# Adaptive max pooling: each load as one contiguous block of the input, outputs in 4 KB rows

## The chip, the core and the metric

The kernel runs on one core of a Trainium2 chip. The core's VectorE (DVE) does all the arithmetic here; SyncE (SP) and ScalarE (ACT) only issue transfers; 16 DMA engines, shared by all queues of the core, move the data between the memory of the chip (DRAM in the profile's names) and SBUF, the on-chip memory of 128 partitions. The metric is the device time of one execution in microseconds (us), as the median of several runs. The profile is of one execution, and its span goes from the first to the last instruction.

## The reference

The input `x` has the shape 32 x 256 x 4096 in float32 (134.22 MB), and the output 32 x 256 x 256 (8.39 MB). Each output is the maximum of a window of 16 neighbouring inputs:

```python
for i in range(output_size):
    start = int(i * length / output_size)
    end = int((i + 1) * length / output_size)
    result[:, :, i] = np.max(x[:, :, start:end], axis=-1)
```

As 4096 is 16 x 256, the windows neither overlap nor cross a row. The whole input can be seen as one flat list of 2,097,152 windows of 64 bytes, in the order of the outputs. Each of the 128 partitions has to handle 16,384 of them, and which ones it handles is free.

## The kernel before

The kernel works on the flat list of windows (`xw`, line 51) and the flat list of outputs (`ow`, line 52). A number of windows `n` in the code always means `n` per partition: 64 n bytes of input and 4 n bytes of output in each partition.

**Two groups.** The function `group` (line 64) takes the next n x 128 windows of the list and cuts them into 128 equal consecutive pieces, one per partition. Group A holds 13,436 windows per partition, group B the other 2,948. So in group A the data of two neighbouring partitions lies 13,436 x 64 = 859,904 bytes apart in DRAM (the "860 KB" row pitch), and in group B 188,672 bytes.

**Loads.** A group is read in several loads, each a column range of that picture: for every partition one run of up to 65,536 bytes, 128 runs in all, a row pitch apart. There are 17 loads: one of 128 windows (`FIRST`, 8,192 bytes per partition), twelve of 1024 (65,536 bytes) and one of 1020 from group A, then two of 1024 and one of 900 (`last`) from group B. Group A is read from the end of its rows to their start, group B from start to end. All loads are issued by SP (lines 87 and 96), in order, on one queue.

**The ring.** The loads land in the tile `ring`, which has room for two loads of 1024 windows and a little more (`GAP`, 152 windows, for each). A load is reduced by two instructions of DVE (line 101, by the helper `pooled`, whose recorded line is 56): one over 872 windows, then one over 152. In every second pass through the ring a load lies 152 windows further along, so it never covers the 152 windows of the old load that the second instruction reads: it has to wait only for the 872-window instruction of the load two before it. In the steady state there is one load moving and the next one queued behind it.

**Outputs.** The maxima go to the tile `kept`, in which each partition has one row of 15,484 outputs. The maxima of the last load (900 per partition) go into `ring` itself, to a place whose data has been read already. At the end come three stores. ACT stores the 900 last outputs per partition (line 114) when the last reduction is through. SP stores the 13,436 outputs per partition of group A, and then the 2,048 others of group B (line 117). In DRAM the outputs of one partition are consecutive within its group, so these three stores have one run per partition each: 53,744, 8,192 and 3,600 bytes. `tc.no_sync_barrier()` stands ahead of SP's stores so that the stores come behind all loads on SP in the program's order. On SP, the store of group A is issued right behind the last load.

**Order.** SP executes its list strictly in order: a load that waits for DVE holds up all that stands behind it. DVE does the reductions in the order of the loads. The framework puts the semaphore waits in; at the very end SP waits for all outstanding transfers (line 148 in the profile).

Of the kernel before, what the change touches and what calls it, by code (L numbers as in the profile page):

```python
# [1 line left out]

# [4 lines left out]


@with_exitstack
def kernel(  # L10
    ctx: ExitStack,
    tc: tile.TileContext,
    x: bass.AP,
    output_size: bass.AP,
    out: bass.AP,
):

    nc = tc.nc
    P = nc.NUM_PARTITIONS
    fp32 = mybir.dt.float32

    B, C, L = x.shape
    O = int(output_size)  # L30
    assert L % O == 0, (L, O)
    W = L // O
    total = B * C * O // P
    assert B * C * O % P == 0

    CHUNK = 1024
    GAP = 152
    FIRST = 128
    LOADS_A, LOADS_B = 13, 2

    LESS = 4
    group_a = [FIRST] + [CHUNK] * (LOADS_A - 1) + [CHUNK - LESS]
    last = total - sum(group_a) - LOADS_B * CHUNK
    group_b = [CHUNK] * LOADS_B + [last]
    assert 0 < last and last * (W + 1) <= CHUNK * W

    pool = ctx.enter_context(tc.tile_pool(name="pool", bufs=1))
    ring = pool.tile([P, 2 * (CHUNK + GAP) * W], fp32, tag="ring", name="ring")
    kept = pool.tile([P, total - last], fp32, tag="kept", name="kept")

    xw = x.flatten_outer_dims().rearrange("r (o w) -> (r o) w", w=W)
    ow = out.flatten_outer_dims().rearrange("r o -> (r o)")

    def pooled(dst, at, n):

        nc.vector.reduce_max(  # L56
            out=dst,
            in_=ring[:, at * W : (at + n) * W].rearrange("p (n w) -> p n w", w=W),
            axis=mybir.AxisListType.X,
        )  # L60

    taken = 0

    def group(n):

        nonlocal taken
        span = slice(taken * P, (taken + n) * P)
        taken += n
        return (
            xw[span].rearrange("(p n) w -> p (n w)", p=P),  # L70
            ow[span].rearrange("(p n) -> p n", p=P),
        )

    stores = []
    n_loads = 0
    base = 0
    for g, loads in enumerate((group_a, group_b)):
        xg, og = group(sum(loads))
        a = sum(loads) if g == 0 else 0
        for n in loads:  # L80
            if g == 0:
                a -= n
            xn = xg[:, a * W : (a + n) * W]
            dst = kept[:, base + a : base + a + n] if n != last else None
            if n == FIRST:

                nc.sync.dma_start(  # L87
                    out=ring[:, CHUNK * W : (CHUNK + n) * W], in_=xn
                )
                pooled(dst, CHUNK, n)  # L90
            else:

                low = n_loads % 2 * (CHUNK + GAP)
                moved = n_loads // 2 % 2
                at = low + moved * GAP
                nc.sync.dma_start(out=ring[:, at * W : (at + n) * W], in_=xn)
                if n != last:
                    cut = CHUNK - GAP if moved else GAP
                    parts = [(0, cut), (cut, n)]
                    for u, v in parts if moved else parts[::-1]:  # L100
                        pooled(dst[:, u:v], at + u, v - u)
                else:
                    end = (at + CHUNK) * W
                    last_kept = ring[:, end - n : end]
                    pooled(last_kept, at, n)
                n_loads += 1
            if g:
                a += n
        full = a - last if g else sum(loads)
        stores.append((og[:, 0:full], kept[:, base : base + full]))  # L110
        base += full
    assert taken == total

    nc.scalar.dma_start(out=og[:, full : full + last], in_=last_kept)
    tc.no_sync_barrier()
    for dst, src in stores:
        nc.sync.dma_start(out=dst, in_=src)


# [1 line left out]
_INS = ['x', 'output_size']  # L121
_OUTS = [((32, 256, 256), 'float32')]

_NUMBERS = {'output_size': 256}


# [26 lines left out]
```

## Time and profile before

| | us |
|---|---|
| time, median of 3 runs (lowest, highest) | 334.98 (334.96, 335.02) |
| span of the profiled execution | 333.06 |
| DVE busy, 32 reductions | 276.5 |
| DVE idle ahead of a reduction, 16 times, all for a load | 51.5 |
| one reduction of 872 windows per partition | 14.69 |
| one reduction of 152 windows per partition | 2.68 |
| the last reduction, of 900 windows per partition | 15.14 |
| a full load, from issue to landing (median) | 24.0 |

The profiled execution has its span of 333.06 us from the first to the last instruction; a timed run is 1.92 us longer at the median, which is what lies around the span. The DMA engines moved 142.61 MB, 428 GB/s over the span. The profile counts as packets the single contiguous runs (one per partition and transfer here) and the 4-byte writes by which each of the 16 engines counts a transfer's semaphore. The records of the single packets have a size, a start and a duration; each engine handles one packet at a time, and 8 of the 128 runs of a transfer. An "issue to landing" time includes the time that a transfer stands behind others in its queue.

### The profile page before, as it was taken

What the parts mean: (1) busy time and instruction counts of PE and PEld (TensorE: products, weight loads), DVE (VectorE), ACT (ScalarE), POOL (GpSimd) and SP (SyncE); (2) the same over time, 40 slices, a digit from 0 to 9 for tenths busy, and PEclk for the clock granted to TensorE, in tenths of its full rate; (3) what the DMA queues carried; (4) which work ended last, traced back from release to release, by engine and by line L of the source; (5) the groups of instructions that cost most, each with busy time, mean ns of one, the idle gap of its engine ahead of it and who ended that gap; (6) DMA issues with size and microseconds to landing.
All of it is one profiled execution on the core that took longest, in us unless ns stands there. A gap on an engine that the chain in (4) does not pass through costs nothing.

```text
span 333.1 us, 113 instructions
## 1 busy us (share of the span) xinstructions
DVE 276.5 (83%) x32; POOL 0.2 (0%) x4
## 2 busy tenths in 40 slices
DVE  2009979797997979799797979979797998979993
POOL 0000000000000000000000000000000000000000
DMA  9898989899898989899898989899898989899996
GB/s 378 378 504 378 504 378 496 386 441 441 378 504 378 504 378 496 386 457 425 378 504 378 504 378 504 378 441 441 385 494 377 504 378 504 378 458 443 421 413 285
DMA packets 2880, 142.61 MB, mean 428 GB/s; under 512 B 320, under 2 KB 320, under 8 KB 448
## 3 DMA queue, kind: packets, MB, share of 16 engines
q1 hardware_dynamic: 2736, 142.15, 98.8%
q10 hardware_dynamic: 144, 0.46, 0.3%
HBM read 134.22 MB, written 8.39 MB: 428 GB/s over the span
## 4 chain that ended last, share of the span: by engine, by line
DMA 57%; DVE 36%; DVEq 5%; issue 0%; SPq 0%
DMA ring<-in_x_dram 57%; DVE kept L56 36%; DVEq L148 5%; SPq L87 0%
## 5 line engine op out<-in xcount | busy, mean ns | idle before, releaser
L56 DVE TENSOR_REDUCE kept<-ring 128x152 f32<-128x2432 f32 (+3 forms) x31 | 261.4, 8472 | 51.5 <-DMA ring<-in_x_dram 51.5
L56 DVE TENSOR_REDUCE ring<-ring 128x900 f32<-128x14400 f32 x1 | 15.1, 15144 | 0.0
L134 POOL MEMSET const-bfloat16-1.0<- 128x1 bf16 x1 | 0.1, 102 | 0.0
L134 POOL MEMSET const-uint8-127<- 128x1 uint8 x1 | 0.1, 102 | 0.0
L134 POOL MEMSET const-float32-0.0<- 128x1 f32 x1 | 0.1, 99 | 0.2 <-issue 0.2
L134 POOL MEMSET const-float32-1.0<- 128x1 f32 x1 | 0.1, 99 | 0.0
## 6 DMA issues: line engine op xcount, KB each, us to landing
ring<-in_x_dram SPq DMA_DIRECT2D x1, 8160.0 KB, 23.9
ring<-in_x_dram SPq DMA_DIRECT2D x1, 7200.0 KB, 21.6
out_dram<-kept SPq DMA_DIRECT2D x1, 6718.0 KB, 37.2
ring<-in_x_dram SPq DMA_DIRECT2D x1, 1024.0 KB, 4.7
out_dram<-kept SPq DMA_DIRECT2D x1, 1024.0 KB, 18.1
out_dram<-ring ACTq DMA_DIRECT2D x1, 450.0 KB, 4.2
ring<-in_x_dram SPq DMA_DIRECT2D x14, 24.0
```

The costliest lines, as they stand in the source:

```text
L56: nc.vector.reduce_max(out=dst, in_=ring[:, at * W : (at + n) * W].rearrange("p (n w) -> p n w", w=W), axis=mybir.AxisListType.X,)
L134: nc = _bacc.Bacc("TRN2", target_bir_lowering=False, num_devices=1)
L148: with _tile.TileContext(nc) as tc:
```

## The change

The groups go. Each load takes the next consecutive block of the flat list of windows and cuts that block into 128 pieces, one per partition. So a load of 1024 windows reads one block of 8 MB without a gap, and neighbouring partitions' runs are 65,536 bytes apart, each beginning where the one before it ends. The sizes become 128, fifteen times 1024, and 896 (`last`) windows per partition. Loads are still 128 runs of up to 65,536 bytes each, issued by SP in order; the places in the ring, the cutting into 872 and 152 windows and the order of the reductions are as before (`place` and the loop over `LOADS`).

In the output, the maxima of one load of 1024 windows now form one block of 512 KB, in which each partition owns 4,096 bytes. The tile `kept` has the loads' outputs side by side in each partition. A store of several loads thus has one run of 4,096 bytes per partition and load. There are four stores: ACT's of the last load (3,584 bytes per partition); on SP those of the first 13 full loads (13 runs of 4,096 bytes per partition), then of `FIRST` (512 bytes per partition), then of the last two full loads (2 runs of 4,096 bytes per partition). The first of SP's stores stands right behind the last load again.

```diff
-    LOADS_A, LOADS_B = 13, 2
-    LESS = 4
-    group_a = [FIRST] + [CHUNK] * (LOADS_A - 1) + [CHUNK - LESS]
-    last = total - sum(group_a) - LOADS_B * CHUNK
-    group_b = [CHUNK] * LOADS_B + [last]
+    LOADS = 15
+    LATE = 2
+    last = total - FIRST - LOADS * CHUNK
...
-    def group(n):
+    def block(n, many=1):
...
-        span = slice(taken * P, (taken + n) * P)
-        taken += n
+        span = slice(taken * P, (taken + n * many) * P)
+        taken += n * many
         return (
-            xw[span].rearrange("(p n) w -> p (n w)", p=P),
-            ow[span].rearrange("(p n) -> p n", p=P),
+            xw[span].rearrange("(l p n) w -> l p (n w)", p=P, n=n),
+            ow[span].rearrange("(l p n) -> p l n", p=P, n=n),
         )
...
+    xf, of = block(FIRST)
+    nc.sync.dma_start(out=ring[:, CHUNK * W : (CHUNK + FIRST) * W], in_=xf[0])
+    pooled(kept[:, 0:FIRST], CHUNK, FIRST)
+
+    xl, ol = block(CHUNK, LOADS)
+    xe, oe = block(last)
...
+    def place(i):
+        moved = i // 2 % 2
+        return i % 2 * (CHUNK + GAP) + moved * GAP, moved
+
+    for i in range(LOADS):
+        at, moved = place(i)
+        nc.sync.dma_start(out=ring[:, at * W : (at + CHUNK) * W], in_=xl[i])
+        dst = kept[:, FIRST + i * CHUNK : FIRST + (i + 1) * CHUNK]
+        cut = CHUNK - GAP if moved else GAP
+        parts = [(0, cut), (cut, CHUNK)]
+        for u, v in parts if moved else parts[::-1]:
+            pooled(dst[:, u:v], at + u, v - u)
+
+    at, _ = place(LOADS)
+    nc.sync.dma_start(out=ring[:, at * W : (at + last) * W], in_=xe[0])
+    end = (at + CHUNK) * W
+    last_kept = ring[:, end - last : end]
+    pooled(last_kept, at, last)
+
+    nc.scalar.dma_start(out=oe[:, 0, :], in_=last_kept)
     tc.no_sync_barrier()
-    for dst, src in stores:
-        nc.sync.dma_start(out=dst, in_=src)
+    for lo, hi in ((0, LOADS - LATE), (LOADS - LATE, LOADS)):
+        nc.sync.dma_start(
+            out=ol[:, lo:hi, :],
+            in_=kept[:, FIRST + lo * CHUNK : FIRST + hi * CHUNK].rearrange(
+                "p (l n) -> p l n", n=CHUNK
+            ),
+        )
+        if lo == 0:
+            nc.sync.dma_start(out=of[:, 0, :], in_=kept[:, 0:FIRST])
```

More of the change, by code (lines that the diff above doesn't have):

```diff
@@ L62 @@
     taken = 0
-    def group(n):
+    def block(n, many=1):
         nonlocal taken
-        span = slice(taken * P, (taken + n) * P)
-        taken += n
+        span = slice(taken * P, (taken + n * many) * P)
+        taken += n * many
         return (
-            xw[span].rearrange("(p n) w -> p (n w)", p=P),
-            ow[span].rearrange("(p n) -> p n", p=P),
-        )
[L74 to L111, printed above, removed]
@@ L112 @@
-    assert taken == total
-    nc.scalar.dma_start(out=og[:, full : full + last], in_=last_kept)
-    tc.no_sync_barrier()
-    for dst, src in stores:
-        nc.sync.dma_start(out=dst, in_=src)
+            xw[span].rearrange("(l p n) w -> l p (n w)", p=P, n=n),
+            ow[span].rearrange("(l p n) -> p l n", p=P, n=n),
+        )
+    xf, of = block(FIRST)
+    nc.sync.dma_start(out=ring[:, CHUNK * W : (CHUNK + FIRST) * W], in_=xf[0])
+    pooled(kept[:, 0:FIRST], CHUNK, FIRST)
+    xl, ol = block(CHUNK, LOADS)
```

## The prediction

> **What bounds the kernel now.** I read the page's head first, then stretches of the span with their DMA share, then the DMA queues and issues, the order of time at the end, and last the single packet records of the trace, grouped by size.
>
> ```profile
> span 333.1 us, 113 instructions
> DVE 276.5 (83%) x32; POOL 0.2 (0%) x4
> q1 hardware_dynamic: 2736, 142.15, 98.8%
> q10 hardware_dynamic: 144, 0.46, 0.3%
> DMA 57%; DVE 36%; DVEq 5%; issue 0%; SPq 0%
> ```
>
> DVE is busy for 83%, the 16 DMA engines for 99.1%. The chain of waits names DVE for 36%, and that misleads: a load's issue waits for DVE to free half of the ring, but the load before it is still moving then. The stretches show it (columns: stretch, busy us of DVE and POOL, clock, DMA share, GB/s):
>
> ```profile
> 0.00:5.00 5.00, 0.00 (x0) 0.20 (x4) 1.00 1.00 393
> 5.00:290.00 285.00, 240.57 (x28) 0.00 (x0) 1.00 1.00 432
> 290.00:312.00 22.00, 19.93 (x4) 0.00 (x0) 1.00 0.99 424
> 312.00:333.00 21.00, 15.97 (x2) 0.00 (x0) 1.00 0.90 384
> ```
>
> In the loads the DMA share is 1.00 and DVE has room: 17.28 us of work in a period of 19.35 us. Only the last stretch is not full, and that is its end: the last packet ends at 331.7. The order of time at the end, and the issues:
>
> ```profile
> 290.99 0.33 SPq L96 DMA_DIRECT2D ring<-in_x_dram  x1
> 291.37 21.91 SPq L117 DMA_DIRECT2D out_dram<-kept  x2
> 295.63 17.28 DVE L56 TENSOR_REDUCE kept<-ring 128x872 f32<-128x13952 f32 x2 [2.07 <-DMA ring<-in_x_dram]
> 312.82 15.14 DVE L56 TENSOR_REDUCE ring<-ring 128x900 f32<-128x14400 f32 x1
> 328.00 0.37 ACTq L114 DMA_DIRECT2D out_dram<-ring  x1
> ...
> out_dram<-kept SPq DMA_DIRECT2D x1, 6718.0 KB, 37.2
> out_dram<-kept SPq DMA_DIRECT2D x1, 1024.0 KB, 18.1
> out_dram<-ring ACTq DMA_DIRECT2D x1, 450.0 KB, 4.2
> ```
>
> The large store is issued at 291.4, lies behind the last load in the same queue, and moves from 311.9 to 328.2. The second store follows to 330.6 and ACT's last one to 331.7 (its data lands at 332.2). Packet records, each engine having 8 of every 128: 65,536 B takes 2419 ns (median; mean 2420.6, fastest 2415, 1792 of them); 57,600 B 2131 (mean 2150); 53,744 B, a store, 1985; 8,192 B 309; 3,600 B, a store, 141. Summed over all data packets and divided by 16 they give 330.0 us, and from the first packet's start (1.7) to the last one's end (331.7) it is 330.0 us. So the engines never stand still: time before is 1.7 us, plus the sum of packet times, plus 1.4 us to the end of the span. What changes no packet's duration and does not starve the queue changes nothing.
>
> The sum is made against this execution's 333.06 us; the median of the three timed runs, 334.98, is 1.92 us more, and that is carried over. A difference under 0.2%, 0.67 us, cannot be told from no change: "same" is 334.31 to 335.65.
>
> **The change part by part.**
>
> Loads, bytes and rows. Before, per partition: 8,192, 14 x 65,536, 65,280 and 57,600 B; after: 8,192, 15 x 65,536 and 57,344 B. The same bytes in the same 17 packets, issued in the same order on SP behind the same waits on DVE: 0 us.
>
> Loads, row pitch. No load of before has a 64 KB pitch. Two pitches are in the trace: 859,904 B (mean of a load's 65,536 B packets 2419.2 to 2423.3 ns) and 188,672 B (2421.5 in both loads). A pitch 4.6 times smaller moved the packet by under 2 ns, inside the spread of the loads at one pitch. Each engine has 120 such packets, plus 8 nearly as long, so 1 ns on all is worth 0.13 us. Lower end: every packet at the fastest seen, 2415, and FIRST's packets all at 309 (its first 16, from a cold start, took 618 on average, in all 0.42 us per engine too much): -0.72 - 0.42 = -1.1 us. Upper end: each of the 17 loads meets that cold price once per engine, 17 x 0.31 = +5.3 us. I take 0, by the row that is nearest in pitch.
>
> Stores. Before, per engine: 8 x 1986 = 15.89 us, 8 x 311.9 = 2.50 us, 8 x 143 = 1.15 us; 19.53 us in 24 packets. After: 15 rows of 4,096 B per partition, one of 512 B, one of 3,584 B, 136 packets. No 4,096 B packet is in the trace; the line through 3,600 B (141) and 8,192 B (309) gives 159 ns: 120 x 159.1 = 19.10 us. The same line gives 28 ns for 512 B, 8 x 28 = 0.22 us; 3,584 B stays at 8 x 143 = 1.14 us. Sum 20.46, that is +0.93 us. Ends: without any price per packet 4,096 B would take 151 ns (the long packets' 0.0368 ns per byte), which takes 1.0 us off; if all took 17 ns more, as the slowest 3,600 B packet did (158 against 141), it adds 2.0 us. I take 159, because 3,600 B is a store to this same output, and only 14% shorter.
>
> Here a rule is weighed. The rows say that a packet costs 7 to 9 ns beside its bytes (6.9 from 53,744 and 65,536 B, 9.3 from 3,600 and 8,192 B); 112 more packets are 0.77 to 1.04 us, which agrees with the 0.93. The Trainium skill, page "DMA: Bandwidth & Descriptors", section "Why small descriptors are slow (HBM only)", puts about 3 cycles of fixed bus cost on each packet; with the 850 MHz that the page gives for the fabric that is an estimate of 3.5 ns, and 112 packets would add only 0.4 us. The rows here do not bear that out, they show twice as much.
>
> Issue of the stores. Store A now has 128 x 13 = 1664 rows instead of 128. SP's issue of a 128-row DMA takes 0.33 to 0.43 us. For 1664 rows it lies between that and 13 times as much, 5.5 us. I take the upper end, and it costs 0: it begins at 291.4, the queue reaches store A only at 311.9, and behind it on SP stand just the 512 B store (0.4 us) and store B, whose wait for DVE ends at 312.9 anyway. Without this cover it would be 5 us.
>
> A fourth store, one more semaphore. Its completions cost 9 ns per engine. In the closing waits on SP, each step that finds its semaphore set takes 0.067 us (331.124 to 331.191). Store B now lands last, not ACT's store, and its semaphore is likely to be first in that row instead of third: +0.13 us; between 0 and that.
>
> DVE and the tail. The last reduction has 896 instead of 900 outputs: 15.14 x 4/900 = 0.07 us less, off the path: ACT's store is then issued at 327.9, its packets begin some 2.2 us later (as 328.0 to 330.24), and 1.15 us of them alternate with store B's until the engines run out of bytes at 331.7 + 0.9 = 332.6. Some 1.3 us of cover; beyond it each us late is a us on the end.
>
> Sum: 0 + 0.93 + 0.01 + 0.13 = +1.07 us; span 334.1, time 334.98 + 1.07 = 336.05 us, +0.3%.
>
> **The rivals.**
>
> B, the 64 KB pitch slows the loads: 16 engines stand in rows that begin at multiples of one power of two, and meet in the same part of the memory. For it: nothing in the trace excludes it, since both pitches of before are odd multiples of 256 B. Against it: packets sit at one flat duration, 2418 to 2427 for nine in ten, for both. Price: from +0.5 us (4 ns a packet) to +5.3 us (the cold price per load), so 336.6 to 341.4, with half of it at about 338.7. The Trainium skill, same page, section "Latency and other measured facts", reports such a loss for copies with row pitches of 512 KiB (slight) to 8 MiB (half the rate), and names contiguous tiles as a cure; no run here shows either, and its smallest pitch is eight times this one.
>
> C, the packet's own price is smaller than the line says, at 4,096 B under 4.8 ns instead of 7 to 9 (then 112 x 4.8 + 0.13 = 0.67 us), or the loads give half a us back. 334.9 to 335.65, no difference. For it: durations are recorded only to some ns. Against it: three pairs of sizes give 7 ns or more. The page's 3 cycles would end here.
>
> D, the row generator becomes the bound: engines take a 4,096 B row every 159/16 = 9.9 ns; if SP's queue hands them out more slowly than that and cannot store them up during the 20 us before, the end is paced by it. At 12 ns per row 1920 rows add 4 us, at 20 ns 19 us: 340 to 355. Against it: 0.43 us for 128 rows is 3.3 ns per row.
>
> E, the other side: contiguous blocks are read faster. Place: the 65,536 B packets. To end below 334.31 it must bring 1.74 us, 13.6 ns of each of 128 packets, so 2407 ns or less; none of the 1792 was under 2415.
>
> **How the numbers follow.** My forecast A, loads unchanged and 0.8 to 1.0 us more in the stores, has 0.54; its own range, with 0.35 us either way for the loads (2.7 ns, the slowest load's mean), is 335.5 to 336.5, and 0.06 of it lies under 335.65. B has 0.22, C 0.12, D 0.07, E 0.05. Slower: 0.48 + 0.22 + 0.07 = 0.77. Same: 0.06 + 0.12 = 0.18. Faster: 0.05. The range 335.1 to 341.0 leaves out E (0.05), C's lower part (0.03), nearly all of D (0.06) and B's top (0.04): 0.18.
>
> **What would show it.** Right: 65,536 B packets still at 2419, 4,096 B ones at 159, DMA share 1.00 up to about 332.6, DVE's idle time before each load's reduction still 2.07 us. B shows in that idle time growing and in packets over 2425; C in 4,096 B packets at 155 or less; D in a DMA share well under 1.00 after 312 or in store A's issue taking over 20 us; E in packets under 2410. A hole between the last load's packets and store A's, or ACT's store beginning after 331.5, would make the sum wrong at the tail.

## The result, and the profile after

The changed kernel takes 335.75 us (median of 9 runs, 335.43 to 336.01) against 334.98 us (334.88 to 335.12): 0.77 us more, a ratio of 1.0022 with a 95% interval of 1.0013 to 1.0030. The profiled execution of it has a span of 333.64 us against 333.06 and belongs to the quickest of the nine; a second one, of the same kernel, had 333.96.

The changed kernel's page: the head, the DMA queues, the chain, and the issues (KB each, us from issue to landing).

```profile
span 333.6 us, 114 instructions
DVE 276.5 (83%) x32; POOL 0.2 (0%) x4
DMA packets 4688, 142.61 MB, mean 427 GB/s; under 512 B 336, under 2 KB 464, under 8 KB 2512
q1 hardware_dynamic: 4544, 142.15, 99.0%
DMA 57%; DVE 36%; DVEq 5%; issue 0%; SPq 0%
ring<-in_x_dram SPq DMA_DIRECT2D x1, 7168.0 KB, 21.6
out_dram<-kept SPq DMA_DIRECT2D x1, 6656.0 KB, 37.4
ring<-in_x_dram SPq DMA_DIRECT2D x1, 1024.0 KB, 4.9
out_dram<-kept SPq DMA_DIRECT2D x1, 1024.0 KB, 15.4
out_dram<-ring ACTq DMA_DIRECT2D x1, 448.0 KB, 4.6
ring<-in_x_dram SPq DMA_DIRECT2D x15, 24.0
out_dram<-kept SPq DMA_DIRECT2D x1, 64.0 KB, 37.1
```

Nothing has changed in kind: the same bytes, DVE busy as long as before, the chain alike, the full loads still 24.0 us from issue to landing. Of the difference the page shows only 1808 more packets. The stretches of the changed kernel (stretch, busy us of DVE and POOL, clock, DMA share, GB/s) and its end in order of time:

```profile
0.00:5.00 5.00, 0.00 (x0) 0.20 (x4) 1.00 0.72 249
5.00:290.00 285.00, 240.39 (x28) 0.00 (x0) 1.00 1.00 433
290.00:312.00 22.00, 19.92 (x4) 0.00 (x0) 1.00 1.00 429
313.00:328.00 15.00, 15.00 (x2) 0.00 (x0) 1.00 1.02 422
```

```profile
291.23 0.33 SPq L95 DMA_DIRECT2D ring<-in_x_dram  x1
291.61 0.43 SPq L103 DMA_DIRECT2D out_dram<-kept  x1
292.09 24.18 SPq L110 DMA_DIRECT2D out_dram<-kept  x1
295.88 17.28 DVE L53 TENSOR_REDUCE kept<-ring 128x872 f32<-128x13952 f32 x2 [2.08 <-DMA ring<-in_x_dram]
313.07 15.07 DVE L53 TENSOR_REDUCE ring<-ring 128x896 f32<-128x14336 f32 x1
316.31 1.25 SPq L103 DMA_DIRECT2D out_dram<-kept  x1
328.18 0.38 ACTq L100 DMA_DIRECT2D out_dram<-ring  x1
```

Two lines are to be read twice. A DMA share of 1.02 cannot be a share of time: the recorded durations of neighbouring packets overlap. So it is not quite true that each engine handles one packet at a time. Inside a transfer a packet's record begins 3 to 4 ns before the one ahead of it ends, in long packets too: those of 65,536 B begin every 2416 to 2417 ns and are recorded with 2420. (In the first stretch the low share is only a matter of where a few long packets are counted, by their start.) And the 512 B store's issue on SP took 24.18 us, where other issues take 0.33 to 0.43: I read this as a full queue.

For the sizes I read the single packets, and the landing of each transfer, for which each of the 16 engines counts once; "mean" is the mean of the 16 counts, in us from the span's start.

| mean landing of | before | after | after, second profile |
|---|---|---|---|
| the first load (1 MB) | 5.16 | 5.44 | 5.36 |
| the last full load | 295.34 | 295.70 | 295.63 |
| the last load | 312.45 | 312.73 | 312.79 |
| ACT's store, the last of all | 332.01 | 332.59 | 332.67 |
| from the last load to that | 19.56 | 19.86 | 19.88 |
| ACT's store on the slowest engine | 332.20 | 332.79 | 333.11 |

So there are two losses, one at either end: 0.2 to 0.3 us by the time the first load has landed, 0.3 us between the last load and the last store. What lies between takes as long as before: 19.346 us per load before, 19.351 after. The span ends with the slowest engine, not with the mean. In the second profile the slowest is 0.44 us behind the mean at the end, in the two others 0.2; this gap differs from profile to profile (0.15 to 0.54 us in those with pitches up to 840 KB), so single spans are a blunt measure of losses this small.

### The profile page after: what moved, and what is told of

Same layout as the page of the kernel before. It is cut to its first block, busy times and chain, and to the rows that moved or that the text cites. A ratio compares the mean times of both kernels' runs of the same rounds, so it can differ in the third digit from the quotient of the medians.

```text
span 333.6 us, 114 instructions
## 1 busy us (share of the span) xinstructions
DVE 276.5 (83%) x32; POOL 0.2 (0%) x4
## 4 chain that ended last, share of the span: by engine, by line
DMA 57%; DVE 36%; DVEq 5%; issue 0%; SPq 0%
DMA ring<-in_x_dram 57%; DVE kept L53 36%; DVEq L141 5%; SPq L74 0%
## 5 line engine op out<-in xcount | busy, mean ns | idle before, releaser
L53 DVE TENSOR_REDUCE kept<-ring 128x872 f32<-128x13952 f32 (+2 forms) x31 | 261.5, 8474 | 51.7 <-DMA ring<-in_x_dram 51.7
L53 DVE TENSOR_REDUCE ring<-ring 128x896 f32<-128x14336 f32 x1 | 15.1, 15075 | 0.0
```

Of the source, the lines that this page charges most:

```text
L53: nc.vector.reduce_max(out=dst, in_=ring[:, at * W : (at + n) * W].rearrange("p (n w) -> p n w", w=W), axis=mybir.AxisListType.X,)
```

## The experiments

Two theories stood against each other after that. **S**: the whole loss is the price of 112 more store packets. **L**: the packets cost only 0.4 us, and the rest sits in the contiguous loads, most likely in the cold start. Crossing loads and stores of the two kernels tells them apart.

### The changed kernel again

> The changed kernel once more, unaltered, for its spread and a second profile. Both theories: 335.75 us give or take 0.15 (334.98 before). Theory S (all of the loss is the 112 extra store packets, loads are free): its 4,096 B packets recorded at 159 ns, store packets summing to 20.4 us per engine against 19.5 before, and whatever varies from one execution to the next varies there. Theory L (part of the loss sits in the contiguous loads): the first packets from a cold start again near 950 ns instead of 618, first load landing near 5.6 us instead of 5.44, and the full-size loads at 2420 ns as before.

Measured: 335.72 us (335.49 to 335.91, before beside it 334.98). The first 16 packets took 906 ns on average (940 in the first profile, 618 before), the first load landed at 5.49 at the latest and 5.36 on average, the 65,536 B packets stand at 2420.8 ns. The cold start (the first packet of each engine) is slower both times. But L had the first load landing near 5.6 at the latest, and on the slowest engine it is only 0.05 us behind the 5.44 of before; the loss shows in the mean.

### Contiguous loads, long rows in the stores

```diff
-    for lo, hi in ((0, LOADS - LATE), (LOADS - LATE, LOADS)):
-        ...
+    cut = (FIRST + (LOADS - LATE) * CHUNK) * P
+    end = cut + LATE * CHUNK * P
+    long_a = ow[0:cut].rearrange("(p n) -> p n", p=P)
+    long_b = ow[cut:end].rearrange("(p n) -> p n", p=P)
+    nc.sync.dma_start(out=long_a, in_=kept[:, 0 : cut // P])
+    nc.sync.dma_start(out=long_b, in_=kept[:, cut // P : end // P])
```

> The loads of the changed kernel, and stores of long rows as before (53,760 and 8,192 B per partition, and ACT's 3,584 B). The maxima of all loads but the last are stored in another order than the reference has. Theory S: the loss is gone, 334.98 us give or take 0.1. Theory L: 0.2 to 0.4 us stay, 335.2 to 335.4, with the wider spread of the changed kernel, and the first load's packets still cold at about 950 ns.

Measured: 335.15 us (334.79 to 335.51), 1.0004 of before with an interval of 0.9995 to 1.0013. The difference of the medians, 0.17 us, lies just under L's forecast, and the interval alone does not exclude S. The trace does show the head's loss: first load at 5.37, last load at 312.71 (before: 5.16 and 312.45). It is made good at the tail: 19.38 us from the last load to the last store, where before needed 19.56.

### Loads of before, 4 KB rows in the stores

```diff
-    nc.scalar.dma_start(out=og[:, full : full + last], in_=last_kept)
+    n_k, n_e = CHUNK, 896
...
+    nc.scalar.dma_start(out=oe, in_=last_kept[:, 0:n_e])
...
-    for dst, src in stores:
-        nc.sync.dma_start(out=dst, in_=src)
+    for lo, hi, at in ((0, 13, FIRST), (13, 15, base - 2 * n_k)):
+        nc.sync.dma_start(
+            out=ol[:, lo:hi, :],
+            in_=kept[:, at : at + (hi - lo) * n_k].rearrange("p (l n) -> p l n", n=n_k),
+        )
+        if lo == 0:
+            nc.sync.dma_start(out=of, in_=kept[:, 0:FIRST])
```

> The loads of before with the four stores of the changed kernel (4,096 B rows, one of 512 B, 3,584 B from ACT). Four outputs per partition of the last load are not stored and the rest stands in another order than the reference has. Theory S: the whole loss, 335.75 to 335.9 us (7 to 9 ns per extra packet, as the durations say). Theory L: only 0.4 us of it, 335.3 to 335.5, since the 4,096 B packets of the changed kernel follow each other every 155 ns although each is recorded with 159, which leaves 3.5 to 4 ns per extra packet.

Measured: 335.39 us (335.19 to 335.76), 1.0015 (1.0006 to 1.0024) of before. That is +0.41 us, in L's range and below S's, though the upper end of the interval, 335.78, just reaches S's 335.75. The first load landed at 5.18 on average, as before; from the last load to the last store it took 19.90 us.

The two halves, 0.17 and 0.41, add up to 0.58 of the 0.74 to 0.77 us. With intervals of some 0.3 us either way the rest of 0.2 us is not resolved.

### The changed kernel with the first load as before

```diff
-    nc.sync.dma_start(out=ring[:, CHUNK * W : (CHUNK + FIRST) * W], in_=xf[0])
+    far = 13436
+    xs = xw[0 : far * P].rearrange("(p n) w -> p (n w)", p=P)
+    nc.sync.dma_start(out=ring[:, CHUNK * W : (CHUNK + FIRST) * W],
+                      in_=xs[:, (far - FIRST) * W : far * W])
```

> The changed kernel with one difference: the first load of 1 MB reads 8,192 B rows 859,904 B apart, as before, instead of one block. Its outputs belong to other windows than the reference's there. Theory S: no difference to the changed kernel, 335.75 us. Theory L with the cold start as the place: its first 16 packets back at about 620 ns and 0.2 us gained, 335.5 us. Theory L with the 64 KB pitch of the later loads as the place: 335.75 us, too, though the first packets are quicker.

Measured: 335.40 us (335.13 to 336.20) beside 335.72 of the changed kernel on the same chip. The first packets are back at 670 ns and the first load at 5.17. S expected no difference. The runs of the two kernels overlap (335.49 to 335.91 for the changed one), so the 0.32 us between the medians is likely rather than certain. The start of DVE's first reduction shows the same in the orders of time, in this sequence: before, changed kernel, this run, contiguous loads with long rows.

```profile
5.46 2.29 DVE L56 TENSOR_REDUCE kept<-ring 128x128 f32<-128x2048 f32 x1 [5.46 <-DMA ring<-in_x_dram]
```

```profile
5.63 2.29 DVE L53 TENSOR_REDUCE kept<-ring 128x128 f32<-128x2048 f32 x1 [5.63 <-DMA ring<-in_x_dram]
```

```profile
5.49 2.29 DVE L53 TENSOR_REDUCE kept<-ring 128x128 f32<-128x2048 f32 x1 [5.49 <-DMA ring<-in_x_dram]
```

```profile
5.56 2.29 DVE L53 TENSOR_REDUCE kept<-ring 128x128 f32<-128x2048 f32 x1 [5.56 <-DMA ring<-in_x_dram]
```

DVE waits for the slowest of the 16 engines, so this column shows a little less than the mean landings do. The trace of this run does not carry the gain to its end: its third load lands at 44.19 on average (changed kernel 44.13 and 44.06), and its last load at 312.80 (312.73 and 312.79). In this one execution something slower in between used up the head start; the gain rests on the medians.

### The kernel before with a contiguous first load

```diff
-                    out=ring[:, CHUNK * W : (CHUNK + n) * W], in_=xn
+                    out=ring[:, CHUNK * W : (CHUNK + n) * W],
+                    in_=xw[0 : n * P].rearrange("(p n) w -> p (n w)", p=P),
```

> The kernel before with one difference: the first load of 1 MB reads one contiguous block instead of rows 859,904 B apart (its outputs belong to other windows than the reference's there). If the contiguous first load costs the 0.3 us that giving it back its pitch brought: 335.2 to 335.3 us, first packets near 900 ns, the first load's landings 0.2 us later on average (5.16 before). If that gain was chance or came from the loads behind it: 334.98 us.

Measured: 335.14 us (334.94 to 335.44) beside 334.91, 1.0006 (0.9997 to 1.0015). The size is the forecast one, though the interval just takes in 1. First packets 753 ns, first load at 5.42 on average. With the run above, two exchanges in opposite directions point to 0.2 to 0.3 us for the first load; each alone is at the edge of what the runs resolve.

### The first load with rows 8,448 B apart

```diff
+    far = FIRST + 4
+    xs = xw[0 : far * P].rearrange("(p n) w -> p (n w)", p=P)
-    nc.sync.dma_start(out=ring[:, CHUNK * W : (CHUNK + FIRST) * W], in_=xf[0])
+    nc.sync.dma_start(out=ring[:, CHUNK * W : (CHUNK + FIRST) * W], in_=xs[:, 0 : FIRST * W])
```

> The changed kernel with the first load's rows 8,448 B apart (8,192 B read, 256 B left out) instead of 8,192: nearly the same block of memory, but no power of two between the rows. Its outputs belong to other windows than the reference's there. If the cold start suffers from the power of two: first packets near 620 to 670 ns and 335.4 us, as with 859,904 B. If it suffers from the rows being close together: near 900 ns and 335.75 us, as in the changed kernel.

Measured: 335.75 us (335.57 to 336.10), as the changed kernel; first load at 5.35 on average, first packets 709 ns. Breaking the power of two does not help here. But "rows close together" does not hold as the cause either, by the runs below: the first load landed on average at 5.33 with 860,160 B between its rows, 5.34 with 524,288, 5.28 with 1,048,576 and 5.47 with 1,048,320. Of all pitches tried only 859,904 B gave 5.16 to 5.18 (three profiles). What makes that one quick is open.

### Rows of 512 B in the stores

```diff
+    ROW = 128
+    per = CHUNK // ROW
+    orow = ow[FIRST * P : (FIRST + LOADS * CHUNK) * P].rearrange(
+        "(l p n) -> p l n", p=P, n=ROW)
...
-            out=ol[:, lo:hi, :],
+            out=orow[:, lo * per : hi * per, :],
...
-                "p (l n) -> p l n", n=CHUNK
+                "p (l n) -> p l n", n=ROW
```

> The changed kernel with its two large SP stores cut into rows of 512 B instead of 4,096 B (120 rows per partition, 840 more packets per engine, the same bytes); the outputs stand in another order than the reference has. Price as the recorded durations have it (27 ns for 512 B, 159 for 4,096 B, so 8 x 27 - 159 = 57 ns more per 4,096 B): 120 x 57 = +6.8 us, 342.6 us. Price as the spacing of the 4,096 B packets has it (155 ns, 3.5 to 4.3 ns per packet beside its bytes): +2.9 to +3.6 us, 338.7 to 339.4 us. If the handing out of rows is what limits: more than 343, with the engines idle between packets.

Measured: 342.32 us (342.20 to 342.38), +7.4 us on before and 6.6 on the changed kernel. By its total the theory of the recorded durations is nearly right (342.6 forecast). The trace does not bear it out. The two stretches of that store (columns as above):

```profile
313.00:321.00 8.00, 7.79 (x2) 0.00 (x0) 1.00 1.15 348
324.00:332.00 8.00, 4.47 (x1) 0.00 (x0) 1.00 1.02 290
```

The spacing, the time from one packet's start to the next one's on the same engine, is 16 divided by the packets that start per ns on all engines. In the first stretch packets come every 23.5 ns on each engine, although each is recorded with 27; hence the share of 1.15. From 322 on the spacing grows, and from 324 on they come every 28 ns. So the total is a small price per packet at first, and then a second slowing.

### Rows of 1,024 B in the stores

The edit is the same with `ROW = 256`.

> The changed kernel with its two large SP stores cut into rows of 1,024 B (60 per partition, 360 more packets per engine, the same bytes); the outputs stand in another order than the reference has. In the 512 B run the packets came every 23.5 ns at first (680 rows per us on 16 engines) and from 322 on every 28 ns (565 per us). If 565 per us is how fast rows are handed out, 1,024 B rows (about 42 ns each, 380 per us) never meet it, and only the price per packet is left: 4.1 to 4.8 ns x 360 = +1.5 to +1.7 us over the changed kernel, 337.2 to 337.4, packets evenly spaced to the end. If each packet costs the 7.8 ns that the whole 512 B run makes per packet: +2.8 us, 338.5. If the recorded durations are right (9.3 ns): +3.3 us, 339.1.

Measured: 337.97 us (337.92 to 338.04) beside 335.07, +2.2 us on the changed kernel: more than the price per packet alone, less than the two others. The stretches:

```profile
313.00:327.00 14.00, 14.00 (x2) 0.00 (x0) 1.00 1.09 387
328.00:335.00 7.00, 0.11 (x1) 0.00 (x0) 1.00 0.97 330
```

Up to 327.7 the packets come every 42.3 ns, just as 4.1 to 4.8 ns per packet would have it. After that they are slower here, too (about 340 rows per us instead of 378). That fells my idea that 565 rows per us is the pace at which rows are handed out: here the slowing comes far below it. What causes it is open.

The undisturbed stretches settle the price: 155.0 ns for 4,096 B, 42.3 for 1,024, 23.5 for 512. The line through the first and the last has 0.0367 ns per byte and 4.7 ns per packet, and it gives 42.3 for the middle one. For the change's 112 extra packets that is 0.53 us. The kernel with contiguous loads and long rows had 19.38 us from the last load to the last store, the changed kernel 19.87: 0.49 us.

### The kernel before with LESS = 0

```diff
-    LESS = 4
+    LESS = 0
```

> The kernel before with LESS = 0: groups of 13,440 and 2,944 windows per partition instead of 13,436 and 2,948, so that output rows are 53,760, 8,192 and 3,584 B and begin at multiples of 256 B, and the row pitches of the input are 860,160 and 188,416 B, multiples of 8 KB, instead of odd multiples of 256 B. If the stores gain from their alignment what contig_long_rows' tail shows (19.38 us from the last load to the last landing on average, against 19.56): 334.8 us. If pitches that are multiples of 8 KB slow the loads as 1 MB does: over 335.2 us, with 65,536 B packets over 2430 ns on average. If neither: 334.95 us.

Measured: 334.80 us (334.64 to 334.92) beside 335.07 us (334.95 to 335.27), a ratio of 0.9992 with an interval of 0.9983 to 1.0001. That is the forecast of the first theory; the interval touches 1, so that it is faster is likely rather than proven. From the last load to the last store it took 19.36 us on average against 19.56, as with the other stores of long rows that begin at multiples of 256 B (19.38 with the contiguous loads above, and 19.38 in the 512 KB run below; the 53,744 B rows of before took 19.56 a second time in the run with the contiguous first load). The head is slower (first load at 5.33), but it did not cost what it did in the two exchanges: the last load landed only 0.09 us later than before (312.54 against 312.45), and the 0.27 us between the medians are more than the tail alone gives. So a late first load does not always reach the end in full. This kernel does the whole computation and has the lowest median of all kernels here.

### Row pitches of 512 KB, 1 MB, and 1 MB less 256 B

The three kernels read whole rows of one (or two) groups; the loop over the loads is the changed kernel's. The diffs leave out the first load, the last load and the stores, which use the same rows. The first, with two groups of 8,192 windows per partition:

```diff
+    half = total // 2
+    xr = [xw[g * half * P : (g + 1) * half * P].rearrange("(p n) w -> p (n w)", p=P)
+          for g in range(2)]
...
-        nc.sync.dma_start(out=ring[:, at * W : (at + CHUNK) * W], in_=xl[i])
+        g, b = (0, a) if i < ONE else (1, (i - ONE) * CHUNK)
+        nc.sync.dma_start(out=ring[:, at * W : (at + CHUNK) * W],
+                          in_=xr[g][:, b * W : (b + CHUNK) * W])
```

> Two groups of 8,192 windows per partition: every load has a row pitch of 524,288 B; long rows in the stores (29,184, 24,576, 8,192 and 3,584 B). Half the pitch that cost 24 us. If the loss comes by steps with the power of two: a part of it, 338 to 347 us (the Trainium skill, page DMA: Bandwidth & Descriptors, has 3% at 512 KiB for copies, which would be about 345). If 1 MB is past an edge: 335 to 335.3 us.

The second, with one group:

```diff
+    xr = xw.rearrange("(p n) w -> p (n w)", p=P)
+    orow = ow.rearrange("(p n) -> p n", p=P)
...
-        nc.sync.dma_start(out=ring[:, at * W : (at + CHUNK) * W], in_=xl[i])
+        nc.sync.dma_start(out=ring[:, at * W : (at + CHUNK) * W],
+                          in_=xr[:, a * W : (a + CHUNK) * W])
```

> One group alone: each partition reads its own 1 MB of the input from its start to its end, so every load has a row pitch of 1,048,576 B, a larger power of two than the change's; the stores are long rows (53,760, 8,192 and 3,584 B). If the loads do not care for the pitch, as 64 KB, 184 KB and 840 KB showed: 334.9 to 335.2 us and 65,536 B packets at 2419 ns. If large powers of two cost what the Trainium skill, page DMA: Bandwidth & Descriptors, reports of copies at 512 KiB (3%) and 2 MiB (a quarter): packets at 2.5 us or more and 345 us or more. The first packets from the cold start show the same question by themselves: 620 ns or well over 900.

The third, as it differs from the second:

```diff
+    span = total - 4
+    last -= 4
-    xr = xw.rearrange("(p n) w -> p (n w)", p=P)
-    orow = ow.rearrange("(p n) -> p n", p=P)
+    xr = xw[0 : span * P].rearrange("(p n) w -> p (n w)", p=P)
+    orow = ow[0 : span * P].rearrange("(p n) -> p n", p=P)
```

> The kernel with a row pitch of 1 MB, made 256 B shorter: 1,048,320 B. Each partition leaves out 4 of its windows, 0.02% of the input, and as many outputs. If what cost 24 us is the power of two: gone, 334.9 to 335.2 us, 65,536 B packets at 2420 ns. If it is the mere distance between the rows: 359 us as with 1 MB. If 256 B is too little to part the rows: in between, or 359 as well.

Measured: 335.25 us at 512 KB (1.0005, interval 0.9996 to 1.0014), 358.99 us at 1 MB (1.072, 1.069 to 1.074), and a ratio of 1.042 (1.038 to 1.045) at 1 MB less 256 B, about 349.0 us, whose four runs lie far apart (347.46 to 353.13). So 512 KB came out as if 1 MB were past an edge, 1 MB as the theory of the large power of two had it, and 256 B less in between. The first packets at 1 MB took neither 620 nor 900 ns but 387. The main stretch of each, in this order, with the columns as above:

```profile
5.00:290.00 285.00, 239.96 (x28) 0.00 (x0) 1.00 1.00 433
```

```profile
5.00:290.00 285.00, 220.34 (x26) 0.00 (x0) 1.00 0.99 403
```

```profile
5.00:290.00 285.00, 226.91 (x27) 0.00 (x0) 1.00 1.00 415
```

The engines are busy all the same, but the bytes flow more slowly: at 1 MB the mean 65,536 B packet takes 2580 ns and single ones up to 4736, while the median is still 2420. A share of 1.00 says nothing on the pace. The second load of the 1 MB kernel lands at 31.2 instead of 24.8 us:

```profile
31.20 17.28 DVE L53 TENSOR_REDUCE kept<-ring 128x872 f32<-128x13952 f32 x2 [23.11 <-DMA ring<-in_x_dram]
```

So the loss of rival B exists. Among the powers of two tried it shows at 1 MB and not at 512 KB or 64 KB, and taking 256 B off gives back two fifths of it (13.9 of 24.1 us stay). What in the memory causes it was not tested. The Trainium skill, page "DMA: Bandwidth & Descriptors", section "Latency and other measured facts", has a slight loss at 512 KiB, a larger one at 2 MiB, and says that 192 B of padding is too little; the loads here show no loss at 512 KB, 7% at 1 MB, and agree that a few hundred bytes are too little (here 256 B less, which did give back a part).

## Why the prediction was right, step by step

The forecast, 336.05 us and slower, was right in sign and near the 335.75 measured: +1.07 us forecast, +0.77 measured. That it came so near is in part luck. Three terms were mis-sized, and their errors went opposite ways: the stores and the closing waits were put too high, the first load too low.

**Loads, bytes and rows: 0.** Right in full flow: 19.346 and 19.351 us per load, and DVE's idle time before each reduction is still 2.07 us.

**Loads, row pitch: taken as 0.** Right for the 65,536 B packets (2420.6 before, 2420.7 after). Wrong for the first load: the cold price that I had only as the upper end, for all 17 loads, was met by one. Its landing is 0.2 to 0.3 us late on average, and exchanging that one load moved the median by 0.23 and 0.32 us. I had taken the nearest row in pitch from loads in full flow; the first load starts from rest, and the trace of before showed that state (618 ns against 309). Why the pitch of 859,904 B alone starts quicker is open.

**Stores: +0.93 us.** The recorded durations came out as predicted: 159 ns for 4,096 B, 27 for 512 B, 20.42 us per engine where I had 20.46. Elapsed time did not: from the last load to the last store 19.87 us instead of 19.56, +0.31. What failed is the step before it, "the engines never stand still", by which time is the sum of packet times. The sum over all data packets rose by 1.11 us (330.03 to 331.14), the time from the first packet's start to the last one's end by 0.70 (329.98 to 330.69; in the second profile, whose engines end further apart, it is 331.00). That both agreed before was chance. Counted by engine, the records overlap by 0.45 us in sum before and by 0.87 after, as there are 112 more packets that each overlap by 3 to 4 ns; and the time from the very first start to the very last end is longer than any engine's own time, since they neither start nor end together. In before, these two errors hid each other. The 7 to 9 ns per packet of the recorded durations hold those 3 to 4 ns of overlap. The spacing of packets, not their recorded length, gives their price.

**The rule that was weighed.** I had written that the rows did not bear out 3 cycles per packet (3.5 ns by an estimate from the Trainium skill, page "DMA: Bandwidth & Descriptors", section "Why small descriptors are slow (HBM only)"). The spacing gives 4.7 ns, nearer to the page's rule than to my 7 to 9. Those 0.53 us for 112 packets are in part made good: kernels whose long rows begin at multiples of 256 B spend 0.2 us less in the tail (19.36 to 19.38 against 19.56), and the change's rows begin so too: 0.50 more and 0.19 less make the 0.31. That this is the reason was not tried by itself.

**Issue of the stores: 0, with the cover named.** The cover held, and the mechanism was another. Store A's own issue took 0.43 us, and the 512 B store's behind it 24.18 us, so that store B was issued at 316.3 instead of 312.9. The engines came to it only at about 329, so it cost nothing. A load behind it on SP would have had to wait as long; no run here has one.

**The closing waits: +0.13 us.** This did not come about. On each engine ACT's packets did not alternate with store B's but came after them; ACT's store still landed last, at 332.79 against 331.71, and from there to the end of the span it took 0.85 us, before 0.86.

**The tail of DVE: 0.** Right: 15.07 us, and ACT's store issued at 328.2, in time.

**Rivals.** C came closest in its mechanism, a price per packet under 4.8 ns (the spacing has 4.7), though the reason was the overlap of the records and not their rounding; the loads of before with the change's stores, 335.39 us, end inside its range. B is real, but at 1 MB and not at 64 KB. D: rows came at up to 680 per us, far from binding at the 103 per us that 4 KB rows need. E did not happen: no 65,536 B packet was under 2415 ns.

## What to carry to other kernels

Where DMA is the bound, take the price of short rows from the spacing of packets in an even stretch (here 4.7 ns a packet beside 0.0367 ns per byte), since recorded durations may overlap; a DMA share above 1.00 gives that away. Price the first transfer apart from those in full flow. And a row pitch is worth a look before a layout is chosen: the pitches tried from 64 KB to 840 KB made no difference in full flow, 1 MB cost 7%.

## What the runs showed of the hardware

- SP's queue seems to hold a limited number of rows. In all seven runs with a 512 B store behind store A, its issue went through when 1226 to 1461 rows of store A were still to start, whether these had 512, 1,024 or 4,096 B; until then SP stood still, for 22 to 40 us.
- Store packets of 512 B run evenly for 10 us and those of 1,024 B for 15 us, and then become 10 to 20% slower to the end (23.5 to 28 ns; 42.3 to 47 ns). The cause is not known.
- The first packets from a cold start took 387 to 958 ns on average, with a median of 309 for the rest of the same load, and differ with the row pitch in no order that I can name.
- The records of neighbouring packets of a transfer overlap by 3 to 4 ns while the packets run evenly, at every size from 512 to 65,536 B, so that sums of them run ahead of the time.
